# The first column pair of a Strassen-style up projection: one product moved forward, banks placed by first use, a fixed order on three engines

## The chip, the cores and the metric

The kernel runs on one core of a Trainium2 chip. TensorE (PE in the profile) multiplies, VectorE (DVE), ScalarE (ACT) and GpSimd (POOL) work on tiles, and SyncE (SP) issues the DMAs. Each engine takes its instructions from a queue of its own, in the order that was fixed when the program was built, and waits where an operand or a buffer isn't ready. TensorE writes into eight banks of PSUM, out of which VectorE and ScalarE read. The metric is the device time of the run in microseconds.

## The reference

The program is one streaming step of a two-layer encoder trunk over 1024 prompt rows and 128 sample rows of width 1024, in float32. Layer 0 is a gated linear recurrence, layer 1 differential attention; each is followed by a squared-ReLU MLP, with norms before and after:

```
def _sqrelu_mlp(x, w_up, w_down):
    return jnp.square(jax.nn.relu(x @ w_up)) @ w_down
...
    for l in range(DEPTH):
        a = _rmsnorm(h, norm_g[l, 0])
        ...
        h = h + _rmsnorm(m, norm_g[l, 1])
        f = _sqrelu_mlp(_rmsnorm(h, norm_g[l, 2]), w_up[l], w_down[l])
        h = h + _rmsnorm(f, norm_g[l, 3])
```

The change lies in `x @ w_up`, 1152 x 1024 times 1024 x 4096, which occurs once in each layer: stage one and stage two below.

## The kernel before

**Number format.** A float32 operand is held as a high half (a cast to float32r, ScalarE) and a low half (operand minus high half, VectorE). A product of two operands is three matmuls for each 128 rows of the contraction: high with high, low with high, high with low (`mm3`).

**Seven products instead of eight.** The 1024 prompt rows are two groups of four blocks of 128, the 1024 features two halves: A11 and A12 (blocks 0 to 3), A21 and A22 (blocks 4 to 7). The weights are taken 256 columns at a time, sixteen such pairs to a stage, and cut in the same way. With the sums S1 = A21+A22, S2 = S1-A11, S3 = A11-A21, S4 = A12-S2, and four sums of weights, seven products P1 to P7 of twelve matmuls each give the four output blocks c11, c12, c21 and c22; these go through relu (ScalarE) and a square (GpSimd, `relu2`, line 756) and are stored. `h_sums` builds from them the sums that the down projection wants.

**What comes before.** The output projection `out_proj` works block by block: product, norm (line 655, VectorE), residual (658), a second norm (275), and then the block's row sums with its partner four blocks away, in place: `pair_sums`, lines 678 to 681. `half_T` transposes half a block: four transposes on TensorE into one bank, a cast of the bank to the high half (ScalarE, line 246), a subtraction for the low half (VectorE, line 247), after which the bank is free. A11, A12, A22 and S2 are transposed there, S2's last block (j = 3) after line 680 of block 7. Block 8, the sample rows, is normed last.

**The first pair.** S1, S3, S4 and the sample block can't be transposed earlier, so the first pair of each stage carries their fourteen groups, through two banks called T that take turns. The order in which the code names the work of this pair is a string:

```
                seq = "P1 P2 T S1 P6 S3 P5 S4 P7 smp P3 P4" if i == 0 else "P1 P6 P2 P5 P7 smp P3 P4"
```

T is the split of the second set of weights (s1) into halves, smp the product of the sample rows (bank U, then relu to the tile hs, its square on GpSimd in line 846, two transposes of hs into U, and a copy). P1 goes to bank X, P2 in the first pair to bank Z, P6 and P7 to Y, P5 and P3 to Z, P4 to Y. c22 is added up from Y, P1 and Z (lines 832 and 833), c12 in line 850, c21 in line 865. Behind c22 the next pair's weights (s2) are split (lines 720 and 721) and GpSimd forms their four sums in place (`sums`, lines 735 to 738); after P3 these sums are split (s0) for P6 of the second pair. The weights of the pair after next are loaded (line 729) into the same buffer once that split is done.

**What sets the order.** A scheduler places the instructions of each engine by their dependences and its own costs. `pin` keeps the matmuls and transposes of the up stage on TensorE in the order of the code; on the other engines the scheduler is free. Banks are placed in the order in which the area `B` names them, and a bank that had been another stage's waits for that stage's last reader.

Of the kernel before, what the change touches and what calls it, by code (L numbers as in the profile page):

```python
# [2 lines left out]

# [7 lines left out]
F32R = mybir.dt.float32r  # L11
# [3 lines left out]
ALU = mybir.AluOpType  # L15
AX = mybir.AxisListType
PSUM = bass.MemoryType.PSUM
DRAM = bass.MemoryType.DRAM

P = 128  # L20
D = 1024
# [3 lines left out]
T = NB * P  # L25
# [6 lines left out]
NP = NBP // 2  # L32
# [25 lines left out]
EARLY = {1: (0,), 2: (1,), 6: (2,), 7: (3,)}  # L58
LATE = (0, 4, 1, 5, 2, 6, 3, 7, 8)
PAIR = 2  # L60


def view(ap, off, dims):
# [4 lines left out]
def tile_kernel(ctx, tc, x_prompt, x_sample, cache_k, cache_v, state_hgrn, norm_g, w_hgrn_in,  # L68
# [124 lines left out]
    NW, NWO = 6, 5  # L193

    rsx = {}

    def rstd_of(ss, n, inv_d, pool, y=None):

# [473 lines left out]

    def pair_sums(blk, j, eng):

        e, o = blk[j], blk[j + NP]
        a11, a12, a21, a22 = e[:, 0:512], e[:, 512:D], o[:, 0:512], o[:, 512:D]
        tt = eng.tensor_tensor
        tt(out=a22, in0=a21, in1=a22, op=ALU.add)
        tt(out=a21, in0=a11, in1=a21, op=ALU.subtract)
        tt(out=a11, in0=a22, in1=a11, op=ALU.subtract)  # L680
        tt(out=a12, in0=a12, in1=a11, op=ALU.subtract)
        half_T(a11, aTh[:, j + NP, 0:4], aTl[:, j + NP, 0:4])

    def again(*a, **k):

# [2 lines left out]
    def mlp_up(l, blk, keep):  # L688
        wu = w_up[l].rearrange("(k p) n -> p k n", p=P)
        with ExitStack() as ms, ExitStack() as ls:  # L690
            R = Area(ms, "ur", "wst s0h s0l s1h s1l a4h a1h a1l a3h a3l a4l p1 u2 c0 hs", side="right")
            B = Area(ms, "ub", "X U Y:2 Z:2 T:2", space=PSUM)
            L = []
            SA = {}
            mk = {"A11": (0, 0), "A12": (0, 4), "S2": (NP, 0), "A22": (NP, 4)}
# [1 line left out]
            def bank(tag):  # L697
                return B.tile([P, 512], F32, name=tag, bufs=1)

# [3 lines left out]
                    return aTh[:, o:o + NP, k0 + k, :], aTl[:, o:o + NP, k0 + k, :]  # L703
                return SA[name][0][:, k, :], SA[name][1][:, k, :]

            def s_ops(name, src):

                n = name[1]
                SA[name] = h, lo = (R.tile([P, 4, HT], F32R, name=f"a{n}h", bufs=1),
                                    R.tile([P, 4, HT], F32R, name=f"a{n}l", bufs=1))  # L710
                for j in range(NP):
                    c = slice(j * P, (j + 1) * P)
                    half_T(src(j), h[:, :, c], lo[:, :, c], transpose, lambda n: bank("T"))

            def split(st, n, parts):

# [63 lines left out]
            for i in range(NFP):  # L780
                sets = (raw, tset)
                C = {}
                seq = "P1 P2 T S1 P6 S3 P5 S4 P7 smp P3 P4" if i == 0 else "P1 P6 P2 P5 P7 smp P3 P4"
                for op in seq.split():
                    if op == "P1":
                        X = bank("X")
# [17 lines left out]
                    elif op == "T":  # L804
                        tset = split(st, 1, [(r1, ca), (r0, ca)])
                        sets = (raw, tset)
                        nx = load(1)
                    elif op == "S1":
                        s_ops(op, lambda j: blk[j + NP][:, 512:D])
                    elif op == "S3":  # L810
                        s_ops(op, lambda j: blk[j + NP][:, 0:512])
                    elif op == "S4":
                        s_ops(op, lambda j: blk[j][:, 512:D])
                        for z in range(2):
                            half_T(blk[NBP][:, z * 512:(z + 1) * 512], aTh[:, NBP, 4 * z:4 * z + 4],
                                   aTl[:, NBP, 4 * z:4 * z + 4], transpose, lambda n: bank("T"))
                        keep.close()
                        L.append(Area(ls, "ul", "s2h s2l c:7 hT"))
                    elif op == "P6":
                        Y = bank("Y")  # L820
                        prod(Y, op, sets, True)
# [6 lines left out]
                        prod(Z, op, sets, True)  # L828
                    elif op == "P7":
                        prod(Y, op, sets, False)  # L830
                        c = C["c22"] = cell()
                        add(out=c, in0=Y, in1=p1, op=ALU.add)
                        add(out=c, in0=c, in1=Z, op=ALU.add)  # L833
# [2 lines left out]
                        if nx is not None:  # L836
                            raw = split(nx, 2 * i + 2, [(r0, ca), (r1, ca)])
                            sums(nx, nc.gpsimd)
                    elif op == "smp":
                        U = bank("U")  # L840
                        wh, wl = sets[0]
                        for k in range(KT):
                            mm3(U[:, 0:2 * P], aT_blk(k, NBP), (wh[:, k, :], wl[:, k, :]), k == 0, k == KT - 1, matmul)
                        hs = R.tile([P, 2 * P], F32, name="hs", bufs=1)
                        nc.scalar.activation(hs, U[:, 0:2 * P], AF.Relu)
                        nc.gpsimd.tensor_tensor(out=hs, in0=hs, in1=hs, op=ALU.mult)
                    elif op == "P3":
                        prod(Z, op, sets, False)
                        c = C["c12"] = cell()
                        add(out=c, in0=Z, in1=u2, op=ALU.add)  # L850
                        relu2(c)
                        store(c, "A12", i)
                        pt = U[:, 2 * P:4 * P]
                        for s in range(2):
                            transpose(pt[:, s * P:(s + 1) * P], hs[:, s * P:(s + 1) * P])
                        hT = L[0].tile([P, 2, P], F32, name="hT", bufs=1)
                        nc.scalar.copy(hT, pt.rearrange("p (s t) -> p s t", s=2))
                        for s in range(2):
                            nc.sync.dma_start(out=us_dr[l][s][i], in_=hT[:, s])
                        if nx is not None:  # L860
                            tset = split(nx, 2 * i + 3, [(r1, ca), (r0, ca)])
                    elif op == "P4":
                        prod(Y, op, sets, False)
                        c = C["c21"] = cell()
                        add(out=c, in0=Y, in1=p1, op=ALU.add)
                        relu2(c)
                pend = C
            h_sums(NFP - 1, **pend)

# [688 lines left out]
```

## Time and profile before

| | |
|---|---|
| runs, median of three | 2954.57 us (2954.5 to 2958.21) |
| profiled execution | 2951.5 us, span 2949.6 us |
| mean granted clock of TensorE | 0.991 |
| TensorE busy | 2856.6 us, 97% of the span |
| VectorE, ScalarE, GpSimd busy | 63%, 41%, 23% |
| first pair to second pair, stage one / two | from 756.6 to 805.4 / from 2195.2 to 2238.5 |

The busy shares are means over the whole program; for the change the two stretches in the last row matter. In a timeline each line gives start and duration in microseconds, the engine, the line of the kernel, the operation, out<-in, and in brackets how long the engine had been idle and who ended it. Where lines are merged (x2), the duration runs from the first start to the last end. A matmul's duration overlaps with the next one's, so a product's length is read from start to start.

### The profile page before, as it was taken

How to read it: one execution, taken by the hardware profiler on the slowest of the kernel's cores; microseconds unless marked ns; L12 is line 12 of the kernel's file. 1: busy time of each engine (PE TensorE's matmuls, PEld its weight loads, DVE VectorE, ACT ScalarE, POOL GpSimd, SP SyncE). 2: the span in 40 equal slices, each digit the busy share in tenths (PEclk: the TensorE clock that was granted, in tenths of full speed). 3: DMA queues.
4: the chain of work that ended last, by engine and by line, in shares of the span. 5: the costliest groups of instructions: out<-in, count | busy, mean ns of one | idle time of the engine just before them, and what ended most of it. 6: DMA issues, size and time to landing. Idle time of an engine off the chain costs nothing. (4 is left out here: it accounts for less than half of the span.)

```text
span 2949.6 us, 45368 instructions
## 1 busy us (share of the span) xinstructions
PE 2856.6 (97%) x16897; PEld 2498.0 (85%) x16897; DVE 1855.0 (63%) x3523; ACT 1205.4 (41%) x2597; POOL 669.3 (23%) x558
## 2 busy tenths in 40 slices
PE   7999999989899999999989999998999999999998
PEld 6999999978688887888779999997877888878886
DVE  7777777776644445465875665656685444545567
ACT  5322222343333334443554554556543333434433
POOL 1111111101145442121211110111114454402311
PEclk9999999989999999999999999999999999999999
DMA  4111111142243348587752121313332433577966
GB/s 137 55 53 53 53 53 53 53 149 86 67 140 127 130 152 289 192 282 257 273 167 69 56 78 48 91 45 96 120 107 93 152 129 127 205 258 236 322 198 244
DMA packets 337120, 405.27 MB, mean 137 GB/s; under 512 B 21081, under 2 KB 210690, under 8 KB 336898
## 3 DMA queue, kind: packets, MB, share of 16 engines
q1 hardware_dynamic: 336898, 402.37, 41.3%
q8 instruction: 133, 2.18, 0.3%
q14 instruction: 89, 0.73, 0.1%
HBM read 280.12 MB, written 122.16 MB: 136 GB/s over the span
## 5 line engine op out<-in xcount | busy, mean ns | idle before, releaser
L238 PE MATMUL D<-wh,aTh 128*128 128x512 f32 x896 | 354.7, 396 | 2.8 <-DVE aO L1044 2.8
L238 PE MATMUL D<-wl,aTh 128*128 128x512 f32 x896 | 354.1, 395 | 0.5 <-DVE wl L905 0.5
L238 PE MATMUL D<-wh,aTl 128*128 128x512 f32 x896 | 354.2, 395 | 0.0
L905 DVE TENSOR_TENSOR aTl<-hst,aTh 128x1024 fp32r<-128x1024 f32 x112 | 156.2, 1399 | 186.2 <-ACT aTh L904 177.8
L238 PE MATMUL pj<-whi,aTh 128*128 128x256 f32 x864 | 254.2, 294 | 0.3
L238 PE MATMUL pj<-wlo,aTh 128*128 128x256 f32 x864 | 244.0, 282 | 2.3 <-DVE wlo L182 2.3
L238 PE MATMUL pj<-whi,aTl 128*128 128x256 f32 x864 | 244.1, 283 | 0.0
L904 ACT CAST aTh<-hst 128x1024 fp32r<-128x1024 f32 x112 | 116.7, 1048 | 247.8 <-PE D L238 217.3
L238 PEld LDWEIGHTS D<-wh,aTh 128*128 128x128 f32 x896 | 169.0, 189 | 43.7 <-issue 2.3
L238 PEld LDWEIGHTS D<-wl,aTh 128*128 128x128 f32 x896 | 169.1, 189 | 40.0 <-DVE wl L905 1.0
L238 PEld LDWEIGHTS D<-wh,aTl 128*128 128x128 f32 x896 | 169.1, 189 | 39.4
L238 PEld LDWEIGHTS pj<-whi,aTh 128*128 128x128 f32 x864 | 164.2, 190 | 6.6 <-issue 4.5
L281 PE MATMUL pi<-whi,aTh 128*128 128x256 f32 x576 | 167.1, 290 | 0.7 <-DVE qk L418 0.7
L238 PEld LDWEIGHTS pj<-wlo,aTh 128*128 128x128 f32 x864 | 163.9, 190 | 3.2 <-DVE wlo L182 2.5
L282 PE MATMUL pi<-wlo,aTh 128*128 128x256 f32 x576 | 166.5, 289 | 0.0
L283 PE MATMUL pi<-whi,aTl 128*128 128x256 f32 x576 | 166.3, 289 | 0.0
L238 PEld LDWEIGHTS pj<-whi,aTl 128*128 128x128 f32 x864 | 163.6, 189 | 0.0
L905 DVE TENSOR_TENSOR wl<-wsta,wh 128x1024 fp32r<-128x1024 f32 x112 | 138.9, 1244 | 22.7 <-ACT wh L904 21.2
L756 POOL TENSOR_TENSOR c<-c 128x512 f32<-128x512 f32 x96 | 115.0, 1198 | 166.0 <-ACT c L755 165.4
L755 ACT ACTIVATE c<-c 128x512 f32<-128x512 f32 x96 | 60.7, 632 | 223.1 <-DVE c L833 184.7
L904 ACT CAST wh<-wsta 128x1024 fp32r<-128x1024 f32 x112 | 117.1, 1049 | 77.9 <-PE D L238 28.3
L506 DVE COPY_PREDICATED A<-masks,lv 128x64 f32<-128x64 uint8 x448 | 85.7, 261 | 48.3 <-PE lv L503 44.3
(484 smaller groups left out, 7946.6 us busy)
## 6 DMA issues: line engine op xcount, KB each, us to landing
u_dr<-c SPq DMA_DIRECT2D x224, 256.0 KB, 4.3
hst<-u_dr SPq DMA_DIRECT2D x112, 512.0 KB, 5.4
wsta<-in_w_down_dram SPq DMA_DIRECT2D x96, 512.0 KB, 4.7
wst<-in_w_up_dram SPq DMA_DIRECT2D x32, 1024.0 KB, 6.1
wstb<-in_w_down_dram SPq DMA_DIRECT2D x32, 512.0 KB, 5.1
wstb<-t_dr SPq DMA_DIRECT2D x32, 512.0 KB, 5.3
h_dr<-hb SPq DMA_DIRECT2D x27, 512.0 KB, 2.6
hb<-h_dr SPq DMA_DIRECT2D x27, 512.0 KB, 4.6
```

Source lines behind the costliest of these rows:

```text
L238: pin(nc.tensor.matmul(*a, **k))
L281: matmul(out, lh, rh, start=first, stop=False)
L282: matmul(out, lh, rl, start=False, stop=False)
L283: matmul(out, ll, rh, start=False, stop=last)
L506: nc.vector.copy_predicated(out=view(A[:], o, [(per, 64 // m), (1, m)]), mask=masks[:, li, :].rearrange("p (j i) -> p j i", i=m), data=lv[ ...
L755: nc.scalar.activation(c, c, AF.Relu)
L756: nc.gpsimd.tensor_tensor(out=c, in0=c, in1=c, op=ALU.mult)
L904: nc.scalar.copy(h, st)
L905: vt(out=lo, in0=st, in1=h.bitcast(F32), op=ALU.subtract)
```

## The change

The string of the first pair is replaced. P4, A22's product, stands third, in a bank of its own (Q, a second Y bank), and c21 takes it from there. The transposes of S2's last block move from `pair_sums` into the first pair's T banks, the groups of S1, S3 and S4 are dealt out between the products one by one, and c21 is added before the sample product. The banks are named in order of first use, with another order for each layer. `in_order` ties the instructions that the first pair issues on TensorE, ScalarE and VectorE into the order of the code; GpSimd and the DMA queue stay with the scheduler. All later pairs keep their string.

```diff
+FIRST_PAIR = "T P1 P2 P4 S1:01 S1:2 S2:3 S1:3 S3:0 P6 S3:12 P5 S3:3 S4:0 P7 S4:123 N C22 C21 smp P3"
...
+    order_of = {}
+
+    @contextmanager
+    def in_order():
+
+        traced = nc.cur_bb.bb.instructions
+        have = {id(i) for i in traced}
+        yield
+        for i in list(traced):
+            if id(i) not in have and i.engine in (mybir.EngineType.PE, mybir.EngineType.Activation,
+                                                  mybir.EngineType.DVE):
+                if i.engine in order_of:
+                    tc.add_manual_dep(i, order_of[i.engine].name,
+                                      mybir.DependencyInfo(mybir.DependencyClass.NoSync,
+                                                           mybir.DependencyReason.DATA), reason="order")
+                order_of[i.engine] = i
...
-        half_T(a11, aTh[:, j + NP, 0:4], aTl[:, j + NP, 0:4])
+        if j < NP - 1:
+            half_T(a11, aTh[:, j + NP, 0:4], aTl[:, j + NP, 0:4])
...
-            B = Area(ms, "ub", "X U Y:2 Z:2 T:2", space=PSUM)
+
+            order = "X T_0 Y_0 Y_1 Z_0 T_1 Z_1 U" if l == 0 else "X T_0 Y_0 Y_1 Z_1 U Z_0 T_1"
+            B = Area(ms, "ub", order + " Y:2 Z:2 T:2", space=PSUM)
...
-            def s_ops(name, src):
-
-                n = name[1]
-                SA[name] = h, lo = (R.tile([P, 4, HT], F32R, name=f"a{n}h", bufs=1),
+            srcs = {"S1": (NP, 512), "S2": (0, 0), "S3": (NP, 0), "S4": (0, 512)}
+
+            def s_op(name, j):
+
+                n, (o, k) = name[1], srcs[name]
+                c = slice(j * P, (j + 1) * P)
+                if name == "S2":
+                    h, lo = aTh[:, NP + j, 0:4], aTl[:, NP + j, 0:4]
+                else:
+                    if name not in SA:
+                        SA[name] = (R.tile([P, 4, HT], F32R, name=f"a{n}h", bufs=1),
                                     R.tile([P, 4, HT], F32R, name=f"a{n}l", bufs=1))
-                for j in range(NP):
-                    c = slice(j * P, (j + 1) * P)
-                    half_T(src(j), h[:, :, c], lo[:, :, c], transpose, lambda n: bank("T"))
+                    h, lo = [x[:, :, c] for x in SA[name]]
+                half_T(blk[o + j][:, k:k + 512], h, lo, transpose, lambda n: bank("T"))
...
-                seq = "P1 P2 T S1 P6 S3 P5 S4 P7 smp P3 P4" if i == 0 else "P1 P6 P2 P5 P7 smp P3 P4"
+                first = ExitStack()
+                if i == 0:
+                    first.enter_context(in_order())
+                seq = FIRST_PAIR if i == 0 else "P1 P6 P2 P5 P7 smp P3 P4"
                 for op in seq.split():
...
-                    elif op == "S1":
-                        s_ops(op, lambda j: blk[j + NP][:, 512:D])
-                    elif op == "S3":
-                        s_ops(op, lambda j: blk[j + NP][:, 0:512])
-                    elif op == "S4":
-                        s_ops(op, lambda j: blk[j][:, 512:D])
+                    elif op[0] == "S":
+                        for j in op[3:]:
+                            s_op(op[:2], int(j))
+                    elif op == "N":
                         for z in range(2):
                             half_T(blk[NBP][:, z * 512:(z + 1) * 512], aTh[:, NBP, 4 * z:4 * z + 4],
                                    aTl[:, NBP, 4 * z:4 * z + 4], transpose, lambda n: bank("T"))
                         keep.close()
                         L.append(Area(ls, "ul", "s2h s2l c:7 hT"))
+                    elif op == "P4" and i == 0:
+                        Q = bank("Y")
+                        prod(Q, op, sets, True)
...
                     elif op == "P7":
                         prod(Y, op, sets, False)
+                    if op == "C22" or op == "P7" and i > 0:
                         c = C["c22"] = cell()
                         add(out=c, in0=Y, in1=p1, op=ALU.add)
                         add(out=c, in0=c, in1=Z, op=ALU.add)
...
-                    elif op == "smp":
+                    if op == "smp":
...
-                    elif op == "P4":
+                    elif op == "P4" and i > 0:
                         prod(Y, op, sets, False)
                         c = C["c21"] = cell()
                         add(out=c, in0=Y, in1=p1, op=ALU.add)
                         relu2(c)
+                    elif op == "C21":
+                        c = C["c21"] = cell()
+                        add(out=c, in0=Y, in1=p1, op=ALU.add)
+                        add(out=c, in0=c, in1=Q, op=ALU.add)
+                        relu2(c)
+                first.close()
                 pend = C
```

TensorE, stage one, from the second product to P6 (Z in the first piece is P2's bank; t_8028 to t_8373 are the blocks 4 to 7). Before:

```order
L238 MATMUL Z_8951<-aTl_100,s0h_8921 128x512
L238 MATMUL Z_8951<-aTh_99,s0l_8922 128x512
L235 MATMUL T_8978<-ident_210,t_8028 128x128 x4
L235 MATMUL T_8985<-ident_210,t_8143 128x128 x4
L235 MATMUL T_8992<-ident_210,t_8258 128x128 x4
L235 MATMUL T_8999<-ident_210,t_8373 128x128 x4
L238 MATMUL Y_9006<-aTh_99,s1h_8968 128x512
L238 MATMUL Y_9006<-aTl_100,s1h_8968 128x512
L238 MATMUL Y_9006<-aTh_99,s1l_8969 128x512
```

And now (Y_8969 is P4's bank, Y_9028 P6's, t_7913 is block 3, which holds S2's last sum):

```order
L257 MATMUL Y_8969<-aTl_100,s1h_8928 128x512
L257 MATMUL Y_8969<-aTh_99,s1l_8929 128x512
L254 MATMUL T_8984<-ident_210,t_8028 128x128 x4
L254 MATMUL T_8991<-ident_210,t_8143 128x128 x4
L254 MATMUL T_8998<-ident_210,t_8258 128x128 x4
L254 MATMUL T_9005<-ident_210,t_7913 128x128 x4
L254 MATMUL T_9012<-ident_210,t_8373 128x128 x4
L254 MATMUL T_9021<-ident_210,t_8028 128x128 x4
L257 MATMUL Y_9028<-aTh_99,s1h_8928 128x512
L257 MATMUL Y_9028<-aTl_100,s1h_8928 128x512
```

P4's product has come between P2 and the transposes, and six groups instead of four stand ahead of P6. P2, further up, follows the group of A22's last block, without S2's last group between them.

ScalarE, stage two, from block 8's sum of squares to the casts out of T (the ACTIVATE of c is c11's relu). Before:

```order
L216 ACTIVATE t,ss<-hb 128x1024
L204 ACTIVATE rs_y<-rs_v 128x1
L246 CAST a1h<-T 128x4x128 x2
L798 ACTIVATE c_23760<-c_23760 128x512
L246 CAST a1h<-T 128x4x128 x2
L246 CAST a3h<-T 128x4x128 x2
```

And now:

```order
L235 ACTIVATE t,ss<-hb 128x1024
L223 ACTIVATE rs_y<-rs_v 128x1
L830 ACTIVATE c_23763<-c_23763 128x512
L265 CAST a1h<-T 128x4x128 x3
L265 CAST aTh<-T 128x512
L265 CAST a1h<-T 128x4x128
L265 CAST a3h<-T 128x4x128 x4
```

The relu of c11 went behind two casts out of T, and now stands ahead of all of them; in stage one it stood behind one.

The end of the first pair, stage one: VectorE, from S4's low halves on. Before:

```order
L247 TENSOR_TENSOR a4l<-T,a4h 128x4x128 x2
L247 TENSOR_TENSOR aTl<-T,aTh 128x512 x2
L832 TENSOR_TENSOR c<-Y,p_8948 128x512
L833 TENSOR_TENSOR c<-c,Z 128x512
L850 TENSOR_TENSOR c<-Z,u_9019 128x512
L721 TENSOR_TENSOR s0l<-wst,s0h 128x1024 x2
L865 TENSOR_TENSOR c<-Y,p_8948 128x512
```

And now:

```order
L266 TENSOR_TENSOR a4l<-T,a4h 128x4x128 x4
L266 TENSOR_TENSOR aTl<-T,aTh 128x512 x2
L866 TENSOR_TENSOR c<-Y,p_8949 128x512
L867 TENSOR_TENSOR c<-c,Z 128x512
L750 TENSOR_TENSOR s2l<-wst,s2h 128x1024 x2
L903 TENSOR_TENSOR c<-Y,p_8949 128x512
L904 TENSOR_TENSOR c<-c,Y 128x512
L884 TENSOR_TENSOR c<-Z,u_9041 128x512
```

The two adds of c22 keep their place. Behind them stand now both subtractions of s2, which stood among S4's low halves, then c21's two adds and c12's; the subtractions of s0 follow behind `h_sums`.

GpSimd in the same place, from c11's square on (wst is the sums of weights, c a square). Before:

```order
L802 TENSOR_TENSOR c_8950<-c_8950 128x512
L735 TENSOR_TENSOR wst<-wst 128x4x128
L736 TENSOR_TENSOR wst<-wst 128x4x128
L737 TENSOR_TENSOR wst<-wst 128x4x128
L1189 MEMSET Qx 128x256
L738 TENSOR_TENSOR wst<-wst 128x4x128
L756 TENSOR_TENSOR c<-c 128x512
L846 TENSOR_TENSOR hs<-hs 128x256
L756 TENSOR_TENSOR c<-c 128x512 x2
```

And now:

```order
L834 TENSOR_TENSOR c_8951<-c_8951 128x512
L1229 MEMSET Qx 128x256
L785 TENSOR_TENSOR c<-c 128x512
L764 TENSOR_TENSOR wst<-wst 128x4x128
L765 TENSOR_TENSOR wst<-wst 128x4x128
L766 TENSOR_TENSOR wst<-wst 128x4x128
L785 TENSOR_TENSOR c<-c 128x512
L880 TENSOR_TENSOR hs<-hs 128x256
L785 TENSOR_TENSOR c<-c 128x512
L767 TENSOR_TENSOR wst<-wst 128x4x128
```

Before, all four sums of weights stood ahead of the squares of c22, hs, c12 and c21. Now c22's square is first, then three sums, c21's square, hs, c12's square, and the fourth sum. On TensorE the two transposes of hs stand between P3 and, now, the X of the second pair; on ScalarE the relu of hs stands behind both casts of s2 and the relu of c21.

## Rows read from the trace of the kernel before

**Rows 1.** Windows: length, busy by engine, TensorE clock, DMA share, GB/s.

```profile
756.60:805.40 48.80, 36.40 (x180) 29.81 (x179) 31.77 (x50) 20.73 (x35) 9.08 (x9) 0.86 0.13 43
766.90:772.00 5.10, 5.10 (x14) 3.96 (x13) 4.05 (x9) 1.94 (x4) 0.00 (x0) 0.52 0.87 294
805.40:827.80 22.40, 22.40 (x112) 18.82 (x111) 10.61 (x14) 7.60 (x11) 11.08 (x10) 1.00 0.41 136
2195.20:2238.50 43.30, 34.50 (x179) 27.44 (x178) 30.41 (x48) 20.53 (x35) 8.81 (x8) 0.92 0.15 49
```

**Rows 2.** Waits of TensorE, first pair, stage one: total, times, longest.

```profile
PE pt L242 <- DVE t L680: 5.8, 1, 5.8
PE T L235 <- DVE a4l L247: 4.2, 2, 3.2
...
PE T L235 <- DVE a3l L247: 1.0, 1, 1.0
```

**Rows 3.** Waits of TensorE, first pair, stage two.

```profile
PE pt L242 <- DVE t L680: 4.7, 1, 4.7
```

**Rows 4.** Timeline of TensorE, stage one: start, duration, operation.

```profile
759.81 0.60 PE L242 MATMUL pt<-ident,t 128*128 128x128 f32 x4
...
775.55 0.48 PE L238 MATMUL Y<-aTh,s1h 128*128 128x512 f32 x1
...
796.74 0.28 PE L238 MATMUL U<-s0h,aTh 128*128 128x256 f32 x1
...
805.35 0.39 PE L238 MATMUL X<-aTh,s2h 128*128 128x512 f32 x1
...
808.09 0.40 PE L238 MATMUL Y<-aTh,s0h 128*128 128x512 f32 x1
...
827.78 0.40 PE L238 MATMUL X<-aTh,s1h 128*128 128x512 f32 x1
```

**Rows 5.** Timeline of VectorE, stage one.

```profile
758.04 1.28 DVE L275 SCALAR_TENSOR_TENSOR t<-hb,rs_y,gb 128x1024 f32<-128x1024 f32 x1
...
773.27 0.69 DVE L247 TENSOR_TENSOR a1l<-T,a1h 128x512 fp32r<-128x512 f32 x1
...
787.66 2.36 DVE L721 TENSOR_TENSOR s2l<-wst,s2h 128x1024 fp32r<-128x1024 f32 x2 [0.81 <-ACT s2h L720]
```

**Rows 6.** Timeline of ScalarE, stage one.

```profile
769.08 1.06 ACT L216 ACTIVATE t<-hb 128x1024 f32<-128x1024 f32 x1 [1.16 <-DVE hb L658]
...
785.91 2.01 ACT L720 CAST s2h<-wst 128x1024 fp32r<-128x1024 f32 x2
...
798.46 0.63 ACT L755 ACTIVATE c<-c 128x512 f32<-128x512 f32 x1 [5.12 <-DVE c L833]
```

**Rows 7.** Timeline of GpSimd, stage one.

```profile
788.97 2.18 POOL L735 TENSOR_TENSOR wst<-wst 128x512 f32<-128x512 f32 x1 [13.97 <-DVE s2l L721]
...
791.23 1.27 POOL L736 TENSOR_TENSOR wst<-wst 128x512 f32<-128x512 f32 x1
...
799.16 1.04 POOL L756 TENSOR_TENSOR c<-c 128x512 f32<-128x512 f32 x1 [3.82 <-ACT c L755]
...
805.23 1.47 POOL L756 TENSOR_TENSOR c<-c 128x512 f32<-128x512 f32 x1 [4.36 <-ACT c L755]
...
822.69 0.61 POOL L846 TENSOR_TENSOR hs<-hs 128x256 f32<-128x256 f32 x1 [0.20 <-ACT hs L845]
```

**Rows 8.** Queue of the DMA issues, stage one.

```profile
805.82 0.38 SPq L729 DMA_DIRECT2D wst<-in_w_up_dram  x1
```

**Rows 9.** Timeline of VectorE, stage two.

```profile
2210.79 1.29 DVE L247 TENSOR_TENSOR a1l<-T,a1h 128x512 fp32r<-128x512 f32 x2
```

**Rows 10.** Timeline of TensorE, stage two.

```profile
2212.55 0.48 PE L238 MATMUL Y<-aTh,s1h 128*128 128x512 f32 x1
...
2238.51 0.40 PE L238 MATMUL X<-aTh,s2h 128*128 128x512 f32 x1
...
2260.97 0.40 PE L238 MATMUL X<-aTh,s1h 128*128 128x512 f32 x1
```

More of the change, by code (lines that the diff above doesn't have):

```diff
@@ L1 @@
 import math
-from contextlib import ExitStack
+from contextlib import ExitStack, contextmanager
 import concourse.bass as bass
```

## Prediction

> **What bounds the kernel now.** I read the windows first [rows 1]. From the second pair of an up stage on, TensorE is busy for all of a stretch (22.40 of 22.40 us, granted clock 1.00); the first pair is different: 48.80 us in stage one (layer 0), of which it works 36.40 at a mean clock of 0.86, and 43.30 in stage two (layer 1), of which it works 34.50 at 0.92. So there a saving must be looked for. The waits of TensorE [rows 2, 3] say what is missing: in stage one 5.8 us for the sum in line 680, then 4.2 us, and about one at a time before, in front of transposes into the T banks, for a low half that VectorE takes out of the bank; in stage two 4.7 us for line 680. A wait costs twice: after the 5.8 us TensorE's second product ran 5.10 us at a granted clock of 0.52 (1.2 GHz) [rows 1], while one at full clock takes 2.74, from 805.35 to 808.09 [rows 4]. Last come the timelines, to see what each engine has queued.
>
> **What the change does, step by step, stage one.** All times are us of the trace of before; the new ones are its durations strung along the new order.
>
> Products two and four. The transposes that waited leave the place ahead of the second product. It starts right behind the group at 759.81 [rows 4], at 760.2, and ends at 763.0 at full clock. A22's product follows. Its third matmul needs the low half of the s1 weights; VectorE reaches it after line 275 (from 758.04, 1.28) [rows 5], six half-block operations at 0.6 (two in 1.29, [rows 9]) and four tiny ones, 0.3 together: 763.1, done 764.35 (2.36 for two, [rows 5]). So one microsecond of wait, and the product ends at 766.7.
>
> The T banks. The first bank is emptied by VectorE, and that stands behind the whole end of block 8 (norm, residual, the sum of squares on ScalarE from 769.08 [rows 6], norm again). Of VectorE's work ahead of it only one low half (0.6) goes away, so the first bank comes free at about 773.2 instead of 773.96 [rows 5]. TensorE writes two groups, to 767.5, and waits 5.7. **The wait of 5.8 is not removed; it stands behind one more product.** From there groups go in twos every 2.05: 1.0 of transposes, 1.0 of wait [rows 2]. Six stand ahead of P6 (four before): 773.2+2.05+1.9 gives 777.1, against 775.55 [rows 4]. Then P6, about 3.4 as the clock is still low at its start (780.5); two groups, 0.8; P5, 2.8 (784.1); two groups, 0.8; P7, held 1.0 by S3's last cast and subtraction (788.7); five groups, 0.4 each and two waits of 1.2 (793.1 to 793.4). There U starts, against 796.74 [rows 4]: 3.3 ahead, as the split of the next weights no longer stands among the subtractions (it made the longest wait in [rows 2], 3.2). With U and P3 of together 5.7, and no fourth product behind, the next X could start at 799.2, against 805.35: 6.1 ahead.
>
> The end of the pair. Between P3 and X stand the two transposes of hs, and hs now comes late. Before, it went through ScalarE and GpSimd as soon as U was done. Now the order on ScalarE puts two casts of s2 and the relu of c21 ahead of it, and c21 is added on VectorE behind both subtractions of s2. The chain: last low half out of T 794.8; two adds to 796.0; relu 0.63, two casts 2.01 [rows 6]; low halves done 798.9 and 800.1; c21's two adds 801.4; relu 802.0; relu of hs 802.4. On GpSimd, three sums of weights stand ahead of both squares: line 735 from 798.9, 2.18 (a neighbour on VectorE as before), then 1.27 each plus gaps [rows 7]: 803.7; c21's square 1.04, hs 0.61 [rows 7]: 805.4. So X starts at 805.8, not at 799.2: **a new wait of 6.4 us takes back the 6.1.** The clock falls again, as it did after 5.8: X takes 4.9, and P6 of the second pair starts at 810.7, against 808.09 [rows 4]: 2.6 behind. Had the clock stayed up, little would be won: its weights need c12's square (1.04), the fourth sum (1.27), a cast (1.0) and a subtraction (1.2) behind hs, so 810.1.
>
> The second pair. The load of the third pair's weights goes when the second of these subtractions is done, 811.2 against 805.82 [rows 8], 5.4 late where TensorE is 2.6 late. Its sums on GpSimd end 2.8 later for TensorE, and hs, which was ready at 823.3 [rows 7] for a use at some 824.7 (827.78 [rows 4] less a product and the two transposes), makes it wait about 1.1. The third X: 3.7 us late. From there the load follows from TensorE's own P3 and nothing carries on.
>
> **Stage two.** P2 is freed in the same way (4.7 [rows 3]). But ScalarE has the relu of c11 ahead of all casts out of T, where two casts went first: the first subtraction, at 2210.79 before [rows 9], starts at 2212.0 (norm and c11 to 2210.8, relu 0.63, cast 0.59). TensorE starts at 2195.2 [rows 1]; three products, two groups and 0.7 of wait for block 7's norm bring it to 2204.9, two groups into T to 2205.7, and there it waits some 7. P6 then starts at 2212.7+2.05+1.9, 2216.7 against 2212.55 [rows 10]; U 3.2 late; without the fourth product X could start at 2238.8, as before (2238.51). The same 6.4 for hs, the slow X and 1.1 bring the third X 10.1 late (2260.97 [rows 10]).
>
> **Not seen before.** GpSimd's squares and its fourth sum now run beside the sums of the h operands on VectorE. The nearest rows: line 756 takes 1.47 beside VectorE and 1.04 alone, line 735 2.18 where its like takes 1.27 [rows 7]. Bounds: 0 and 1.8 (two such hits) a stage; I take 0.4, the excess of line 756, which is the nearest operation. Behind this row stands a rule of the Trainium skill ("SBUF — State Buffer", section "SBUF: two separate sides"): GpSimd and a VectorE instruction with two SBUF inputs share one port pair, held for a whole instruction, the other blocked. The 2.18 agrees (1.27 and the 1.0 left of the subtraction). By it both ends of GpSimd's queue are exposed to four sums, and the sum would be nearer the upper bound; if the two shared evenly, nearer mine.
>
> The banks placed by first use let T's first group start without block 8's bank, and P2 of stage two without it; the first is worth nothing while ScalarE and VectorE come late, the second is counted. Bounds 0 to 0.5. Elsewhere the orders are the same, so the rest is 0.
>
> **Sum.** 3.7+10.1+0.8 = 14.6 us. The profiled execution took 2951.5 (span 2949.6), so 2966.1; the median of the runs is 3.07 above it: 2969.2.
>
> **Rivals.**
> - Clock low for longer (0.17). It fell for some 5 us after each wait so far [rows 1]. Here the first wait is followed by transposes with gaps before P6, so all of P6 may run low: 2.4 less the 0.6 counted; with the upper port bound, 1.4 more, that is 3.2 a stage: 2975.6. For: the mean of 0.86 [rows 1]; against: full clock between gaps of 1.0 before.
> - No change (0.09). hs gets ahead: if GpSimd's sums were not in its way, X comes at 804.3 rather than 805.8, and the third pair does not wait; with the T banks free 1.5 sooner as well and no neighbour on GpSimd, 2 x 4.5 less: 2960.2. To be within 0.2% (5.9 us, which is what a measurement can tell) it needs both. Against: the order on GpSimd, and the residual of block 8, which didn't move.
> - Faster (0.06). TensorE gets hs and the next weights by 799.2 and 2238.8: stage one 6.1 gained, stage two 0.3 lost, 2948.8. Decided by the chain from the last T bank to s0's low half, 15.3 us by the rows, being under 7.5; for it speaks that U itself is done 3.3 us earlier; against, no row of these operations is half as long in another place.
>
> **How the numbers follow.** My forecast, 2969, has 0.68, with its own range of 2963 to 2974. The range takes in the port bounds, the low clock and most of the no-change case: 2959 to 2977. Faster by over 0.2% 0.06, within 0.10 (the no-change case and a little of the forecast's edge), slower 0.84.
>
> **What would show it.** In the new profile: TensorE waiting 5 to 7 us for a low half out of the second T group in each stage, and 5 to 7 us for hs from GpSimd in front of its two transposes; P6 of the second pair 2 to 3 us late in stage one and 9 in stage two; no wait for line 680. I am wrong if the transposes of hs don't wait, or if the first pair gets shorter than 43 us in both stages.

## The result and the profile after

The changed kernel takes 2975.05 us (median of 6 runs, 2973.38 to 2978.54), the kernel before, run beside it, 2954.55: a ratio of 1.0068, 95% interval 1.0058 to 1.0079, so some 20 us slower. The forecast was 2969.0, range 2959 to 2977. The profiled execution has a span of 2973.9 us.

Read the first pair and the second of each stage first, in the windows of the changed kernel (columns as in [rows 1]: length, busy time of TensorE, its weight loads, VectorE, ScalarE, GpSimd, clock, DMA share, GB/s):

```profile
756.70:808.90 52.20, 34.91 (x179) 27.98 (x178) 31.84 (x51) 18.98 (x33) 10.00 (x9) 0.87 0.12 41
779.40:782.10 2.70, 2.70 (x9) 2.18 (x9) 1.38 (x2) 0.77 (x2) 0.00 (x0) 0.54 0.00 0
808.90:838.00 29.10, 26.07 (x113) 21.13 (x111) 13.94 (x14) 9.36 (x13) 12.60 (x10) 0.88 0.35 115
2209.40:2260.20 50.80, 34.30 (x179) 27.54 (x178) 30.91 (x49) 18.86 (x33) 8.71 (x8) 0.90 0.12 42
2260.20:2286.50 26.30, 24.41 (x112) 19.90 (x112) 14.06 (x14) 9.27 (x13) 12.89 (x10) 0.94 0.35 120
```

Against [rows 1] the first pair of stage one went from 48.80 to 52.20, the second from 22.40, with no idle time, to 29.10 with three; in stage two the first went from 43.30 to 50.80. TensorE does as many matmuls in the first pair as before (179 records against 180, 34.91 us against 36.40; P4 was last in the pair and is third now), so what grows is its idle time, from 12.4 to 17.3 us. Its waits in stage one, where [rows 2] stood, of both pairs (total, times, longest):

```profile
PE U L254 <- POOL hs L880: 9.4, 2, 6.4
PE T L254 <- DVE a1l L266: 7.9, 2, 7.4
PE T L254 <- DVE a4l L266: 1.8, 2, 1.0
PE Y L257 <- DVE s1l L750: 0.7, 1, 0.7
```

No wait for the sum that stood in line 680. In its place are the two that the prediction named. They stand at these points of TensorE's timeline (start, duration, operation, idle time before it); the second, fourth and last line answer to P6, X and the third X in [rows 4]:

```profile
775.33 1.97 PE L254 MATMUL T<-ident,t 128*128 128x128 f32 x8 [7.36 <-DVE a1l L266]
...
779.47 0.78 PE L257 MATMUL Y<-aTh,s1h 128*128 128x512 f32 x1
...
808.59 0.69 PE L254 MATMUL U<-ident,hs 128*128 128x128 f32 x2 [6.42 <-POOL hs L880]
808.92 0.78 PE L257 MATMUL X<-aTh,s2h 128*128 128x512 f32 x1
...
833.62 0.69 PE L254 MATMUL U<-ident,hs 128*128 128x128 f32 x2 [2.96 <-POOL hs L880]
...
838.00 0.40 PE L257 MATMUL X<-aTh,s1h 128*128 128x512 f32 x1
```

What hs waits for is read from GpSimd (timeline; answers to [rows 7]):

```profile
799.89 1.04 POOL L785 TENSOR_TENSOR c<-c 128x512 f32<-128x512 f32 x1 [3.09 <-ACT c L784]
802.09 2.18 POOL L764 TENSOR_TENSOR wst<-wst 128x512 f32<-128x512 f32 x1 [1.16 <-DVE s2l L750]
...
806.92 1.04 POOL L785 TENSOR_TENSOR c<-c 128x512 f32<-128x512 f32 x1
807.92 0.61 POOL L880 TENSOR_TENSOR hs<-hs 128x256 f32<-128x256 f32 x1
808.49 1.49 POOL L785 TENSOR_TENSOR c<-c 128x512 f32<-128x512 f32 x1
809.94 1.72 POOL L767 TENSOR_TENSOR wst<-wst 128x512 f32<-128x512 f32 x1
```

The sums of weights, which ran from 788.97 in [rows 7], start 13 us later, behind c22's square; three of them and c21's square stand ahead of hs. And what the first bank of T waits for, from VectorE (answers to [rows 5]):

```profile
771.70 1.28 DVE L294 SCALAR_TENSOR_TENSOR t<-hb,rs_y,gb 128x1024 f32<-128x1024 f32 x1
774.59 1.29 DVE L266 TENSOR_TENSOR a1l<-T,a1h 128x512 fp32r<-128x512 f32 x2 [1.60 <-DMA h_dr<-hb]
```

The 1.60 us for a DMA were not foreseen: a1l lies on memory that hb has to leave first, and hb leaves it by its store. In the queue of DMA issues the load of the next weights, 1 MB, stands ahead of that store. It did so before too, but 3.5 us ahead, and a1l didn't wait then; now it is 1.7 us ahead. Before:

```profile
765.48 0.38 SPq L729 DMA_DIRECT2D wst<-in_w_up_dram  x1
769.01 0.33 SPq L659 DMA_DIRECT2D h_dr<-hb  x1
```

And now:

```profile
767.41 0.38 SPq L758 DMA_DIRECT2D wst<-in_w_up_dram  x1
769.15 0.33 SPq L678 DMA_DIRECT2D h_dr<-hb  x1
```

### The profile page after: what moved, and what is told of

Read it like the earlier page. It is cut to its first block, busy times and chain, and to the rows that moved or that the text cites. A ratio compares the mean times of both kernels' runs of the same rounds, so it can differ in the third digit from the quotient of the medians.

```text
span 2973.9 us, 45358 instructions
## 1 busy us (share of the span) xinstructions
PE 2863.2 (96%) x16897; PEld 2500.0 (84%) x16897; DVE 1857.2 (62%) x3525; ACT 1207.6 (41%) x2597; POOL 671.7 (23%) x558
## 5 line engine op out<-in xcount | busy, mean ns | idle before, releaser
L945 DVE TENSOR_TENSOR aTl<-hst,aTh 128x1024 fp32r<-128x1024 f32 x112 | 147.3, 1320 | 188.4 <-ACT aTh L944 179.9
L1353 POOL COPY qq<-q 128x256 f32<-128x256 f32 x64 | 27.8, 435 | 391.3 <-PE pqT L254 260.9
```

Source lines behind the costliest of these rows:

```text
L945: vt(out=lo, in0=st, in1=h.bitcast(F32), op=ALU.subtract)
L1353: nc.gpsimd.tensor_copy(qq, view(Qb[h, i][:], (h % 2) * P, [(64, 2), (0, 2), (1, 64)]))
```

## The experiments

In every group of runs the kernel before ran on the same chip; its median was 2954.7, 2956.7 and 2958.3 us in the three groups, so kernels of different groups are compared by their ratio to it. Beside the times I read from each trace the length of both stages, from the first X to that of the third pair (before 71.20 and 65.76, changed 81.28 and 77.15).

| kernel | median us | ratio, 95% | stage one | stage two |
|---|---|---|---|---|
| changed | 2975.05 | 1.0068 (1.0058-1.0079) | 81.28 | 77.15 |
| banks | 2975.59 | 1.0063 (1.0044-1.0082) | 78.33 | 77.80 |
| smp | 2973.58 | 1.0065 (1.0053-1.0077) | 79.93 | 76.77 |
| load | 2973.59 | 1.0061 (1.0049-1.0073) | 75.74 | 76.96 |
| free | 2970.03 | 1.0054 (1.0042-1.0066) | 76.97 | 73.38 |
| fixed | 2968.23 | 1.0046 (1.0034-1.0058) | 75.39 | 73.24 |
| early | 2966.18 | 1.0035 (1.0023-1.0047) | 76.96 | 75.28 |
| tail | 2965.26 | 1.0032 (1.0020-1.0043) | 74.58 | 72.49 |
| p4 | 2965.09 | 1.0027 (1.0015-1.0039) | 74.15 | 70.12 |
| cast | 2962.25 | 1.0012 (1.0004-1.0021) | 74.92 | 71.48 |
| p4last | 2947.20 | 0.9966 (0.9954-0.9978) | 65.64 | 64.95 |
| best4 | 2945.73 | 0.9962 (0.9950-0.9974) | 65.32 | 63.43 |

**smp: hs ahead of c22 and c21.**

```diff
-FIRST_PAIR = "T P1 P2 P4 S1:01 S1:2 S2:3 S1:3 S3:0 P6 S3:12 P5 S3:3 S4:0 P7 S4:123 N C22 C21 smp P3"
+FIRST_PAIR = "T P1 P2 P4 S1:01 S1:2 S2:3 S1:3 S3:0 P6 S3:12 P5 S3:3 S4:0 P7 S4:123 N smp C22 C21 P3"
```

> The sample product and its square root of evictions (hs) are put ahead of the sums of c22 and c21 in the first pair; all else as in the changed kernel. Theory A (the loss of about 20 us is the whole of the three waits of TensorE per stage, and what stands behind hs on the engines, the split of the next weights, binds nearly as late): the waits of 6.4 us for hs in front of the two U transposes vanish, but a wait of about 5 to 6 us for s0l comes up in front of P6 of the second pair, and the time falls by only 2 to 4 us, to 2971 to 2973. Theory B (hs alone is what TensorE is late for): 2 x 6.4 us come back, 2962 or less, and no wait over 1 us takes their place.

2973.58. The waits for hs are gone, and TensorE stops one product later (its timeline, stage one):

```profile
803.93 0.38 PE L254 MATMUL U<-ident,hs 128*128 128x128 f32 x2
...
812.86 0.79 PE L257 MATMUL Y<-aTh,s0h 128*128 128x512 f32 x1 [5.71 <-ACT s0h L749]
...
815.52 0.80 PE L257 MATMUL Y<-aTh,s0l 128*128 128x512 f32 x1 [1.44 <-DVE s0l L750]
```

Theory A: hs was only the first of a queue that is late as a whole.

**free: a fixed order on TensorE alone.**

```diff
-if id(i) not in have and i.engine in (mybir.EngineType.PE, mybir.EngineType.Activation,
-                                      mybir.EngineType.DVE):
+if id(i) not in have and i.engine in (mybir.EngineType.PE,):
```

> The fixed order is kept on TensorE alone; ScalarE and VectorE are ordered by the scheduler again. P4 third and the new banks stay. Theory A (the fixed order on ScalarE and VectorE makes hs and the next weights late): both waits for hs vanish or fall under 1 us, the wait for a1l in front of the T transposes (7.4 and 6.8 us) stays, because the first sum still waits behind P4 and the evictions: 2952 to 2960. Rival B (moving P4 third costs by itself, whatever stands on the other engines): 2965 or more, with a T wait of 7 us and a new wait of some us behind it. Rival C (the fixed order costs nothing): within 2 us of 2975.

2970.03: theory A fell. The waits for hs went (1.4 at most are left), but in stage one 5.70 us for a4l came up instead, because on VectorE the split of s2 and parts of c22 and c21 now stand among the subtractions that empty the T banks:

```profile
795.00 1.22 DVE L749 TENSOR_TENSOR s2l<-wst,s2h 128x1024 fp32r<-128x1024 f32 x1
...
796.74 1.91 DVE L749 TENSOR_TENSOR s2l<-wst,s2h 128x1024 fp32r<-128x1024 f32 x1
798.57 0.67 DVE L866 TENSOR_TENSOR c<-c,Z 128x512 f32<-128x512 f32 x1
799.16 1.28 DVE L265 TENSOR_TENSOR a4l<-T,a4h 128x512 fp32r<-128x512 f32 x2
```

The wait for a1l stayed (6.16 and 6.39). Rival B was right on the time.

**load: the next weights behind hb's store.**

`d` is the load, `stored[0]` block 8's store; the lines that set them are left out.

```diff
...
+if i == 1:
+    tc.add_manual_dep(d.ins, stored[0].ins.name,
+                      mybir.DependencyInfo(mybir.DependencyClass.NoSync,
+                                           mybir.DependencyReason.DATA), reason="order")
```

> The load of the second pair's weights is put behind the store of block 8's hb in the queue of SP; nothing else moves. Theory A (a1l's tile lies on hb's memory, and hb's store lands late because the 1 MB load runs ahead of it): the wait of 1.60 us of VectorE's a1l for h_dr<-hb in stage one falls under 0.3 us, TensorE's wait for a1l falls from 7.4 to about 5.7 us, the first T transposes start 1.6 us earlier, and stage one ends 1 to 2 us earlier; stage two is unchanged: 2973 to 2974. Rival B (the store lands when it does because of its own issue time, 769.15 us, and not because of the load): the wait of 1.6 us stays, 2975.

VectorE no longer waits for hb's store, TensorE waits 5.85 instead of 7.36, and P6 now starts at a granted clock of 1.00 and not 0.54: the first pair is 2.7 us shorter (49.50 from X to X against 52.20), more than the 1 to 2 expected. Stage one is shorter by 5.5, but the other 2.8 are not shown to come from this edit. They lie in the second pair (26.24 against 29.08), which waits 0.89 for hs instead of 2.96, and there the load of the third pair's weights took 5.55 us from its issue to the first cast where it had taken 7.12. The kernel banks below, whose issues stand as in the changed kernel, has 5.60 and a second pair of 26.28; the changed kernel's own stage two has 5.59 and 26.27. The changed kernel first, then banks:

```profile
815.33 0.38 SPq L758 DMA_DIRECT2D wst<-in_w_up_dram  x1
822.45 2.00 ACT L749 CAST s1h<-wst 128x1024 fp32r<-128x1024 f32 x2 [8.18 <-DMA wst<-in_w_up_dram]
...
814.50 0.38 SPq L758 DMA_DIRECT2D wst<-in_w_up_dram  x1
820.10 2.00 ACT L749 CAST s1h<-wst 128x1024 fp32r<-128x1024 f32 x2 [6.75 <-DMA wst<-in_w_up_dram]
```

In the times the gain can't be seen: 2973.59, with an interval of the ratio that overlaps the changed kernel's, and the profiled run was the fastest of six.

**fixed: the kernel before with the fixed order alone.**

`in_order` is the changed kernel's, and is left out here.

```diff
...
+if i == 0:
+    first.enter_context(in_order())
```

> The kernel before, its order of products and its banks, with one part of the change alone: a fixed order on TensorE, ScalarE and VectorE in the first pair. Theory A (the fixed order is most of the loss, but it loses by what it puts behind what, and in this string hs stands ahead of the sums): hs waits small, the split of s1 stands behind the relu and sum of c11, so P6 of the first pair and the first T transposes come 1 to 3 us later, and s0l stands ahead of c21: 2957 to 2963. Rival B (a fixed order costs about what the changed kernel loses wherever it stands): 2970 to 2975. Rival C (it costs nothing): within 2 us of 2954.6.

2968.23, between the two. In this string the split of s1 follows c11; on VectorE it stands ahead of a1l and itself waits:

```profile
769.87 0.68 DVE L817 TENSOR_TENSOR c<-Z,p 128x512 f32<-128x512 f32 x1
772.19 2.37 DVE L738 TENSOR_TENSOR s1l<-wst,s1h 128x1024 fp32r<-128x1024 f32 x2 [1.63 <-ACT s1h L737]
774.48 0.68 DVE L264 TENSOR_TENSOR a1l<-T,a1h 128x512 fp32r<-128x512 f32 x1
```

So TensorE waits 5.8 and 6.2 for a1l, as in the changed kernel but for another operation.

**p4: the kernel before with P4 third alone.**

```diff
-seq = "P1 P2 T S1 P6 S3 P5 S4 P7 smp P3 P4"
+seq = "P1 P2 T P4 S1 P6 S3 P5 S4 P7 smp P3 C21"
...
```

The rest of the edit gives P4 its own bank and adds c21 up from there, as in the changed kernel.

> The kernel before with one part of the change alone: A22's product (P4) stands third in the first pair, and c21 gets its own sum; the transposes of sums, the banks and the free order of ScalarE and VectorE stay as before. Theory A (moving P4 up costs nothing by itself; the loss is what the new string and the fixed order put behind the last transposes): the 5.8 us wait for L680 stays, P4 covers the wait for a1l, P6 comes 2 to 3 us later and X of the second pair within 1 us of before, with at most 2 us of wait for s0l behind it in a stage: 2953 to 2958. Rival B (P4 third costs by itself, as free at 2970 could be read): 2963 or more.

2965.09, 8 us above before by the medians of its group: in the range of B, so P4 third costs by itself in this kernel. The 5.8 for line 680 stays, and X comes 48.74 us after the start of stage one and 43.44 after that of stage two (48.77 and 43.30 before), as A has it. But in both stages the second pair now waits 2.4 us for hs, where it did not wait before. The cast of the weights s0 waits for P3, the last product that reads the old ones. Before, a fourth product stood between P3 and X and gave the cast and the subtraction time; now X follows at once. Before and p4, with X at 805.35 and 805.56:

```profile
802.35 2.00 ACT L720 CAST s0h<-wst 128x1024 fp32r<-128x1024 f32 x2 [2.18 <-PE Z L238]
...
805.41 2.00 ACT L720 CAST s0h<-wst 128x1024 fp32r<-128x1024 f32 x2 [1.92 <-PE Z L238]
```

The load of the third pair's weights, which goes when that subtraction is done, is issued 5.2 us after X instead of 0.5. The last two kernels below differ in P4's place and agree with it: 6.0 us and a wait of 1.6 for hs with P4 third, 2.2 us and no such wait with P4 last.

**tail: the split of the next weights ahead of P7.**

```diff
-FIRST_PAIR = "T P1 P2 P4 S1:01 S1:2 S2:3 S1:3 S3:0 P6 S3:12 P5 S3:3 S4:0 P7 S4:123 N C22 C21 smp P3"
+FIRST_PAIR = "T P1 P2 P4 S1:01 S1:2 S2:3 S1:3 S3:0 P6 S3:12 P5 S3:3 S4:0123 N R P7 C22 C21 smp P3"
```

R holds the split and the sums, which C22 held (the lines that move them are left out).

> The changed kernel with the split and the sums of the second pair's weights (s2h, s2l, wst) put right behind the last transposes, ahead of P7 and of c22's sums, all four transposes of S4 and those of the sample block in front of P7. Theory A (the split stands too late, behind c22; hidden under P7 it costs nothing): the waits of 6.4 us for hs fall to 2 us or less, nothing over 2 us takes their place, the wait for a1l in front of the T transposes stays: 2975 - 2 x 5 = 2965, 2962 to 2968. Rival B (ScalarE, VectorE and GpSimd are bound in this stretch by the sum of their work): the wait moves to s0l or to a4l and the time stays above 2970.

2965.26, as A; but 3.3 us of the waits for hs remain in each stage, as c21's sums still stand ahead of it.

**early: the casts of a1 ahead of c11's sum, and off hb.** C11 in the string is c11's sum and relu, which P2 held; the lines that move them are left out.

```diff
-R = Area(ms, "ur", "wst s0h s0l s1h s1l a4h a1h a1l a3h a3l a4l p1 u2 c0 hs", side="right")
+R = Area(ms, "ur", "wst s0h s0l s1h s1l a1h a1l a4h a3h a3l a4l p1 u2 c0 hs", side="right")
-FIRST_PAIR = "T P1 P2 P4 S1:01 S1:2 S2:3 S1:3 S3:0 P6 S3:12 P5 S3:3 S4:0 P7 S4:123 N C22 C21 smp P3"
+FIRST_PAIR = "T P1 P2 P4 S1:01 S1:2 S2:3 C11 S1:3 S3:0 P6 S3:12 P5 S3:3 S4:0 P7 S4:123 N C22 C21 smp P3"
```

> The changed kernel with c11's sum and relu moved behind the first casts of a1, and a1h and a1l each one place further to the right, so that a1l no longer lies over hb. Theory A (the wait for a1l of 7.4 and 6.8 us is the chain of block 8's norm, plus c11's relu 0.5, plus hb's store 1.6 in stage one): in stage one VectorE's wait for h_dr goes and the wait for a1l falls to 4.5 to 5.5 us; in stage two it falls by 0.5 to 1 us; the waits for hs stay at 6.4: 2970 to 2973. Rival B (the transposes would wait for something else as long): no change, 2975.

2966.18, 4 us below A's lower end. The waits for a1l fall to 5.44 and 4.91, those for hs stay at 6.42 and 6.43. The two stages of its trace are 6.2 us shorter than the changed kernel's, the medians 9; the rest is not explained. What is left of the first wait is block 8's norm, as cast shows below.

**banks: the placement of before.**

```diff
-order = "X T_0 Y_0 Y_1 Z_0 T_1 Z_1 U" if l == 0 else "X T_0 Y_0 Y_1 Z_1 U Z_0 T_1"
+order = "X U"
```

> The changed kernel with the banks placed as before (X and U first, the order by first use undone). Theory A (the placement frees no bank that anything waits for): the same waits, within 2 us of 2975. Rival B (a bank's last reader in the stage ahead holds the first writer back in one of the placements): a wait of 1 us or more at the first X, Z or T of a stage, and 1 to 5 us.

2975.59, so no change in time, though rival B's wait is there. In stage two TensorE's waits are

```profile
PE U L254 <- POOL hs L880: 7.0, 2, 5.5
PE Z L257 <- DVE t L674: 5.6, 1, 5.6
PE T L254 <- DVE a1l L266: 1.8, 2, 1.0
```

P2 waits 5.6 for a bank that the stage ahead still reads, and then at most 1.0 for a1l. The new placement moves one wait behind two products and shortens nothing.

**cast: block 8's square behind the first casts of a1.** As early, and (the lines that note the square and the cast are left out)

```diff
...
+if op == "S1:01":
+    tc.add_manual_dep(sq8[0], last_cast[0].name,
+                      mybir.DependencyInfo(mybir.DependencyClass.NoSync,
+                                           mybir.DependencyReason.DATA), reason="order")
```

> The kernel early with one order more: ScalarE's square of block 8's hb is put behind the first two casts of a1, which are ready before it. Theory A (the wait for a1l is block 8's norm standing ahead of the casts on ScalarE and VectorE, and nothing in the data): the wait for a1l falls from 5.4 and 4.9 us to 1 to 2 us in both stages and the transposes and P6 behind it come 4 us earlier; the 6.4 us for hs stay: 2966 - 2 x 3.5 = 2959, 2956 to 2962. Rival B (block 8's norm, now later, makes the last transposes late by as much): a new wait of 2 us or more in front of N's transposes, 2964 or more.

2962.25, at the edge of A. TensorE's timeline in stage one:

```profile
770.08 1.25 PE L256 MATMUL T<-ident,t 128*128 128x128 f32 x8 [1.80 <-DVE a1l L270]
```

1.80 and, in stage two, 1.29 where 7.36 and 6.77 stood. Nothing in the data kept the first casts waiting but their place behind block 8, and no wait of 2 us came up at N. The 6.4 for hs stays.

**best4: all repairs, P4 third, the engines still in a fixed order.** cast and tail, and

```diff
-FIRST_PAIR = "T P1 P2 P4 S1:01 S1:2 S2:3 S1:3 S3:0 P6 S3:12 P5 S3:3 S4:0 P7 S4:123 N C22 C21 smp P3"
+FIRST_PAIR = "T P1 P2 P4 S1:01 S1:2 S2:3 C11 S1:3 S3:0 P6 S3:12 P5 S3:3 S4:0123 N R P7 C22 smp C21 P3"
-nc.gpsimd.tensor_tensor(out=hs, in0=hs, in1=hs, op=ALU.mult)
+(nc.vector if i == 0 else nc.gpsimd).tensor_tensor(out=hs, in0=hs, in1=hs, op=ALU.mult)
...
```

Besides, s0's split stands ahead of hT's copy, and h_sums of the first pair joins the fixed order behind it.

> All repairs together, P4 still third and the three engines still in a fixed order: the first casts of a1 ahead of block 8's square, c11's sum behind them, a1l off hb, the split of the next weights ahead of P7, the sample product ahead of c21's sums, hs squared on VectorE, s0's split ahead of hT's copy and of h_sums. Theory A (the fixed order costs by what it puts behind what, and not as such): the waits for a1l and hs fall to 2 us each or less, stages of 64 to 68 us: 2943 to 2953, faster than both kernels. Rival B (the sum of the work on ScalarE, VectorE and GpSimd binds this stretch): waits of 3 us or more turn up for a4l, s0l or hs, 2955 to 2962.

2945.73, ratio 0.9962: faster than both kernels. Windows (first pair, second pair, first pair of stage two) and TensorE's waits in stage one:

```profile
757.20:796.40 39.20, 33.30 (x178) 26.86 (x177) 30.49 (x50) 17.95 (x32) 7.40 (x6) 0.96 0.14 47
796.40:822.50 26.10, 23.19 (x113) 18.75 (x112) 13.91 (x15) 10.32 (x15) 14.02 (x12) 1.00 0.39 132
2189.30:2226.60 37.30, 31.95 (x179) 25.63 (x179) 29.47 (x49) 17.84 (x32) 7.12 (x5) 1.00 0.15 50
```

```profile
PE T L256 <- DVE a1l L270: 2.6, 2, 1.8
PE U L256 <- POOL hs L894: 1.6, 1, 1.6
PE T L256 <- DVE a4l L270: 1.6, 2, 0.8
PE Y L259 <- DVE s0l L756: 1.3, 1, 1.3
```

The first pair is 13.0 us shorter than in the changed kernel, of which TensorE's own work gives 1.6, by the clock; the rest is waits.

**p4last: best4 with P4 last again.**

```diff
-FIRST_PAIR = "T P1 P2 P4 S1:01 S1:2 S2:3 C11 S1:3 S3:0 P6 S3:12 P5 S3:3 S4:0123 N R P7 C22 smp C21 P3"
+FIRST_PAIR = "T P1 P2 S1:01 S1:2 S2:3 C11 S1:3 S3:0 P6 S3:12 P5 S3:3 S4:0123 N R P7 C22 smp P3 P4 C21"
...
```

P4 is added into Y again, and c21 needs one sum less.

> best4 with P4 back at its old place behind the sample product and P3, so that it is again added into Y and c21 needs one sum less. Theory A (P4 third fills the wait for block 8, and P4 last covers hs and s0l: once the casts come early the place in front is worth little): within 3 us of best4. Rival B (with P4 out of the front TensorE waits 3 us longer for a1l, and the clock falls): 4 to 8 us above best4.

2947.20, as A; the intervals of the two ratios overlap. TensorE now waits 5.58 and 4.14 for a1l, but no more for hs or s0l, in either pair. Where P4 stands fills one wait or the other.

## Why the prediction was right, and where it was short

The time lies in the stated range, 2 us below its upper end, and 1 us above the forecast's own range (2963 to 2974). The two waits are the ones that were forecast; the size of stage one was too small.

- **The wait of 5.8 stands behind one more product.** Right; and early and cast show by what: c11's relu, block 8's norm and, in stage one, the store of hb ahead of the first casts and subtractions.
- **A new wait of 6.4 for hs.** 6.42 and 6.43 measured. smp shows that it is not hs by itself, and tail that the place of the split, behind c22, makes half of it; 3.3 are left there, behind c21's sums.
- **The signs.** The wait for a1l was forecast as 5 to 7 us in each stage: 7.36 and 6.77. P6 of the second pair came 5.3 us late in stage one (forecast 2 to 3) and 9.05 in stage two (forecast 9).
- **Stage two, third X 10.1 late, 0.4 for the port.** 11.4 measured (77.15 less 65.76). P6 was forecast at 2216.7; it came at 2231.33, or 2217.2 once the later start of the stage (14.2) is taken off.
- **Stage one, third X 3.7 late, 0.4 for the port.** This is the term that was too small: 10.1 measured (81.28 less 71.20). Half of the miss is in the first pair, X 3.4 late and not 0.45, and load shows by what. The wait for a1l was 7.36 and not 5.7: it ended on the store of hb, which "the residual of block 8, which didn't move" left out. Behind the longer wait the transposes took 1.97 for eight where 1.0 was counted, and P6 came at 779.47, not 777.1. In load, which takes the wait for the store away alone, X comes 0.7 late. The other half is in the second pair, 6.65 us longer than before where 3.25 was forecast: hs was late by 2.96 and not 1.1 (the forecast's own numbers give 1.4), and the product behind it took 4.04 (833.96 to 838.00), the first 2.3 of them at a granted clock of 0.50, against 2.88 before. In banks, load and stage two the same pair is 3.8 longer, as the load of the weights there takes 5.6 us and not 7.1. So nearly all of this half is a slow transfer in the profiled execution, for which no run shows a cause. With it and the store taken out, load's stage one is 4.5 late, close to the forecast's 4.1.
- **The port, 0.4 a stage.** GpSimd's square beside VectorE took 1.49 and its fourth sum 1.72, where 1.04 and 1.27 are the times alone: 0.9 ahead of s0h. VectorE's sums beside them took 1.08, 1.42 and 1.76, against 0.69 for the one that ran alone:

```profile
809.11 1.42 DVE L799 TENSOR_TENSOR c<-c,c 128x512 f32<-128x512 f32 x1
810.45 1.76 DVE L800 TENSOR_TENSOR c<-c,c 128x512 f32<-128x512 f32 x1
812.30 0.69 DVE L801 TENSOR_TENSOR c<-c 128x512 f32<-128x512 f32 x1
```

  The Trainium skill ("SBUF — State Buffer", section "SBUF: two separate sides") has one of the two engines hold the shared pair for a whole instruction while the other is blocked; that both columns grow agrees with it, but would also be so if the two shared evenly, so the rule is not decided here. The measured 0.9 lies between the bounds of 0 and 1.8. TensorE itself waited 0.4 us for s0l in stage two, and under 0.1 in stage one, where the first 3.6 us of X ran at a granted clock of 0.50 meanwhile.
- **The clock.** The rival of a clock low for longer had 2975.6, the time that was measured, but not by its mechanism: it wanted 3.2 us more in each stage, and stage two has 0.9 more than forecast. In stage one the clock added to a longer wait.
- **From the sum to the median.** The two stages are 21.5 us longer by the traces, the medians 20.5 apart. Stage two starts 14.2 late, 10.1 of them from stage one. I don't count the 4 between as the change's: no edit names work of that stretch, and its length against before goes from -0.8 (early) to +6.9 (p4). With one trace for each kernel this is a reading and not shown.

What stays open: how much of a stage's length changes from run to run, as each kernel has one trace, and why the third pair's load took 7.1 us in three of them (changed, early, cast) at a place where it took 5.6 in others. So the sum of the stages and the ratio agree only within some 6 us for a kernel. Two parts of the change, S2's last transposes in the first pair and the groups dealt out one by one, were not run alone; best4 and p4last keep both and are faster than the kernel before.

## What to carry to other kernels

A wait in front of a product is filled by another product only if what ends the wait doesn't stay where it is: find the instruction that the wait ends on, and what stands ahead of it on its own engine, before moving the work of the engine that waits. A fixed order need not cost time: best4 keeps it and is the fastest, though no run has best4's repairs without it. What costs, in a fixed order or a free one, is work that nobody waits for yet (c11's relu, a norm) ahead of what empties a bank, or work that is needed a pair later (the split of the next weights) taken out of the gaps that hid it. When one late operation is moved ahead, look at what stood behind it: smp brought hs forward and s0h was late instead. A product that is moved forward also leaves its old place: P4 last had given the next weights the time to be split. And before a gain in a trace is put down to an edit, look whether its place is one that the edit touches: half of load's gain in stage one came with a transfer that was as short in a kernel without the edit.

## What was not expected of the hardware

- Memory that is used again was held until a store had landed, not until it was issued: hb's 512 KB store, issued at 769.15, 1.7 us behind a 1 MB load, held VectorE until 774.59; issued ahead of the load (load), or 3.5 us behind it (before), it held nobody.
- The same 1 MB load, issued 6.4 us after X with the same issues ahead of it, took 7.12 us to the first cast in the changed kernel and 5.60 in banks; the 1.5 us became 2.8 in the second pair, as the product behind the longer wait started at a granted clock of 0.50 and in banks at 1.00.
- Waits cost more than their length through TensorE's clock: eight transposes took 1.97 us after the 7.36 us wait and 1.25 after one of 1.80 (cast), and the first 2.7 us of P6 behind them had a granted clock of 0.54, the level of 1.2 GHz. In load, with a wait of 5.85 there, P6 started at 1.00. The clock over the first pair of stage two was 0.90 in the changed kernel and 1.00 in best4.
